# A hybrid encoder's first stage: the sample's projection taken on x * w, with rstd at the readout

## The chip, the cores and the metric

The kernel runs on one core of a Trainium2 chip. The metric is device time in microseconds (us) of the whole kernel. Five engines work from queues of their own, each in program order: TensorE (PE, matrix products), VectorE (DVE), ScalarE (ACT), GpSimd (POOL) and SyncE (SP), which issues most DMAs. They wait for each other by semaphores. TensorE writes its sums into PSUM banks; all other tiles lie in SBUF, "on chip" below.

## The reference

Two requests share one set of weights: a prompt of 1024 tokens and a sample of 256 tokens, each of width 1024. One layer follows: a token-mixing block, cross-attention into 256 memory tokens, and a feed-forward part. Only the start of the first block matters here:

```
h = rmsnorm(x, norm_mix_w)            # x * rsqrt(mean(x*x) + eps) * w
proj = h @ w_in                       # split into qkv, ab, dn_gate, sg_u, sg_v, gate_a, gate_b
u = gelu(sg_u); v = layernorm(gelu(sg_v))
y_b = (u * (w_s @ v + b_s)) @ w_up_b  # w_s mixes the tokens of a chunk of 128
```

`rsqrt(mean(x*x) + eps)` is one number per token, called rstd here. It can be applied to `x` before the product or to the product's rows after it.

## The kernel before

Tokens form three blocks: 0 and 1 are the two halves of the prompt (512 tokens each), 2 is the sample (256 tokens). A chunk is 128 tokens. Activations lie with features on the partitions: a tile `x[:, k, :]` is 128 features by the block's tokens, `k` from 0 to 7 (`KT` = 8).

Every product is made of three: both operands are split into a rounded high part and the remainder (`hi`, `lo`), and `hi*hi`, `lo*hi` and `hi*lo` are summed in one bank. `split` (L124) makes the high part on ACT (L125) and the remainder on DVE or POOL (L126). For weights the two parts are `svh`/`svl` (the `w_sv` halves) and `whi`/`wlo` (all the others); `raw` is a weight tile as loaded.

The stage around the change runs in this order on TensorE:

- `sgv(2)`, the sample's columns `sg_v` and `ab`: two halves of the weight (264 columns each), two chunks, 24 products of 264 columns for each pair: 96 in all.
- `bias()`, one product that needs the small tile `sw`.
- `sgu(0, 2)` and `sgu(1, 2)`, the sample's first two groups of `sg_u`: 24 products of 256 columns each.
- `sgv(0)`: the same as `sgv(2)` for the four chunks of block 0, 192 products; then `sgu(0, 0)` and `sgu(1, 0)`, 24 products of 512 columns each; then `sgv(1)`, and so on.

The norms run beside it. A norm squares `x` on ACT (L240, L243), adds the squares on DVE (L244, the tile `nacc`), sums over the partitions with products of one column (`bank<-cst,nacc`), takes rsqrt on DVE in three rounds of three small instructions (L226 to L228, the tile `nst`), spreads the result over the partitions with products of 128 columns (`bank<-cst,nst`), and then for each `k` multiplies on DVE (L276, the tile `nt`) and splits into `hi` and `lo` (L287: odd `k` have their remainder on DVE, even `k` on POOL). `nt` and the squares share three rooms. After each readout of a bank, `gelu2` (L400) runs ACT, DVE, ACT, DVE in turn.

The order on TensorE is written out by hand, with generators: the main one emits products, and side ones (the norms, the layer norm `ln`, the mixing products) are resumed when a planned clock, advanced by each product's planned time, reaches a due time. `LAG0` is such a time: how far behind the start of block 0's norm its column sums are placed. The other engines get their order from a scheduler within the same program. `x` of block 1 is loaded into the room of block 0's `x`, so its load waits for the last `nt` of block 0.

Of the kernel before, what the change touches and what calls it, by code (L numbers as in the profile page):

```python
# [54 lines left out]
class Trunk:  # L55
# [68 lines left out]
    def split(self, hi, lo, src, eng=None):  # L124
        self.nc.scalar.activation(hi, src, AF.Copy)  # L125
        (eng or self.nc.vector).tensor_tensor(out=lo, in0=src, in1=f32(hi), op=ALU.subtract)  # L126
# [37 lines left out]
def trunk_kernel(ctx: ExitStack, tc: tile.TileContext, a):  # L164
# [122 lines left out]
    def to_h(h, b):  # L287
        return lambda k, t: split(h[b][0][:, k, :], h[b][1][:, k, :], t, V if k % 2 else G)

    def act_tiles(p=None):  # L290

        p = p or hp
        return [
            (
                p.tile([P, KT, n], F32R, tag=f"hi{b}", name=f"hi{b}"),
                p.tile([P, KT, n], F32R, tag=f"lo{b}", name=f"lo{b}"),
            )
            for b, (_, n) in enumerate(BLOCKS)
        ]
# [29 lines left out]
            SY.dma_start(x[:, k : k + 2, :], src[:, k : k + 2, t0 : t0 + n])  # L329
        return x  # L330

    def sv_raw(half):
        raws = [K.raw() for _ in range(2)]
        for i, raw in enumerate(raws):
            SY.dma_start(raw, a["w_sv"][half][:, i * 1056 : (i + 1) * 1056])
        return raws

    def sv_split(half, raws):
        lo = svp.tile([P, 8 * 264], F32R, tag="lo", name="svl")
        hi = svp.tile([P, 8 * 264], F32R, tag="hi", name="svh")  # L340
        for i, raw in enumerate(raws):
            sl = slice(i * 1056, (i + 1) * 1056)
            split(hi[:, sl], lo[:, sl], raw, V if i else G)
        sv.append((hi, lo))


    xs = hp.tile([P, KT, NS], F32, tag="lo1", name="xs")
    for k in range(0, KT, 2):
        SY.dma_start(xs[:, k : k + 2, :], a["xT"][:, k : k + 2, NP:])
    SY.dma_start(sm, a["small"])  # L350
    SY.dma_start(cst[:, C_BD:], a["const"][:, C_BD:])
    sv_raw0 = sv_raw(0)
    SY.dma_start(cst[:, :C_BD], a["const"][:, :C_BD])
    x_h = act_tiles()

    def first_norm():

        nm = Norm(xp, 512)
        for k in range(0, KT, 2):
            nm.add(xs[:, k : k + 2, :].rearrange("p k t -> p (k t)"))  # L360
        nm.n = NS
        yield from nm.rest(lambda k: xs[:, k, :], S_MIX, to_h(x_h, 2), 0, lag=0, halves=2)

    first = K.side(first_norm())
    sv_split(0, sv_raw0)
    x0 = x_load(a["xT"], 0, 512, "x0")
    sv_split(1, sv_raw(1))
    K.finish(first)

    done = set()  # L370

    def other_norms():
        yield from norm(xp, lambda k: x0[:, k, :], 512, S_MIX, to_h(x_h, 0), 600, 0, LAG0)
        done.add(0)
        x1_ = x_load(a["xT"], 512, 512, "x1")
        yield 3000
# [62 lines left out]
    def decays():  # L439
# [46 lines left out]
            tr(pt[:, d * 40 : (d + 1) * 40], gr[:, d, :], ident[:40, :40])  # L486
        V.tensor_copy(gcol.rearrange("p d r -> p (d r)"), pt[:, :80])

    def sgv(b):
        if b < 2:  # L490
            K.until(norms, lambda: b in done)
        for half in (0, 1):
            w = sv[half]
            nv = 264 if half == 0 else 248
            for c in range(4 * b, min(4 * b + 4, NCH)):
                cs = slice((c % 4) * P, (c % 4 + 1) * P)
                hi, lo = x_h[b]
                ps = bank(pm)
                n = 0
                for k in range(KT):  # L500
                    wh, wl = wk(w, k, 264)
                    for l, r in ((hi[:, k, cs], wh), (lo[:, k, cs], wh), (hi[:, k, cs], wl)):
                        mm(ps[:, :264], l, r, n == 0, n == 23)
                        n += 1
                    yield 0
                acc = (s0 if half == 0 else s1)[:, c : c + 1]
                gelu2(sp, ps[:, :nv], vg[:, c, half * 264 : half * 264 + nv], nv, acc)
                if half:
                    V.tensor_copy(ab[:, c, :], ps[:, 248:264])
        lns[b] = K.side(ln(slice(4 * b, min(4 * b + 4, NCH))))  # L510
        K.ahead()

    def bias():
# [23 lines left out]
    def sgu(g, b):  # L537
# [10 lines left out]
        gelu2(sp, ps, ug, n)  # L548
        mixes.append(K.side(mix(g, b, ug)))

    for b in (2, 0, 1):
# [6 lines left out]
        K.main(sgu(1, b))  # L558
    for g in (2, 3):
        for b in (2, 0, 1):  # L560
            K.main(sgu(g, b))
# [1553 lines left out]
```

## Time and profile before

| what | us |
|---|---|
| median of 3 runs | 2263.11 |
| lowest and highest run | 2262.23, 2266.95 |
| the profiled execution | 2267.29 |
| its span in the trace | 2265.1 |
| TensorE busy in the span | 2204.3 |
| start of the first product with `w_sv` | 15.04 |
| block 0's rstd spread over the partitions (`bank<-cst,nst`) | 37.31 |
| block 1's column sums (`bank<-cst,nacc`) | 64.53 |
| start of `sgv(1)` | 87.04 |

Times in the trace are counted from the span's start. A row of the timeline gives start, duration, engine, line, operation, out<-in with partitions and elements, and the count of merged instructions; in brackets stands how long the engine was idle before it, and who ended that.

### The profile page before, as it was taken

The numbers are of one execution on the slowest core, as the hardware profiler recorded it, in microseconds if no ns is written. First come the engines' busy times: TensorE is split into PE (matmuls) and PEld (weight loads), VectorE is DVE, ScalarE is ACT, GpSimd is POOL, SyncE is SP. The second block draws the span as 40 slices with busy tenths as digits, with TensorE's granted clock in tenths as the row PEclk, the third lists the DMA queues.
The fourth block names the chain that finished last, engine by engine and source line by source line (L and its number), as shares of the span: only waits on it lengthen the run. The fifth ranks groups of instructions, "written<-read, shape, count | busy, mean of one in ns | idle before, by whom it ended". The sixth has DMA issues, their size and how long they took to land.

```text
span 2265.1 us, 32398 instructions
## 1 busy us (share of the span) xinstructions
PE 2204.3 (97%) x12464; PEld 1923.5 (85%) x12464; DVE 1396.8 (62%) x2774; ACT 815.7 (36%) x1480; POOL 527.5 (23%) x352
## 2 busy tenths in 40 slices
PE   6999999999999999999999999899999999999998
PEld 6988888888888898888888888788888888878888
DVE  7868778897985964664534547543344334468575
ACT  5433243333424433232344423323233222343453
POOL 3010000000000000013221331566666666100031
PEclk9999999999999999999999999899999999999999
DMA  5221322223234555962231431223222222593531
GB/s 186 83 82 62 105 66 85 78 65 98 73 110 125 158 140 166 308 227 94 91 101 47 163 131 59 72 82 114 78 79 89 75 82 75 167 346 110 198 110 56
DMA packets 191301, 262.47 MB, mean 116 GB/s; under 512 B 72410, under 2 KB 102698, under 8 KB 191146
## 3 DMA queue, kind: packets, MB, share of 16 engines
q1 hardware_dynamic: 171306, 231.30, 31.6%
q10 hardware_dynamic: 19840, 29.11, 3.5%
q8 instruction: 97, 1.59, 0.3%
q14 instruction: 58, 0.48, 0.1%
HBM read 182.19 MB, written 78.16 MB: 115 GB/s over the span
## 4 chain that ended last, share of the span: by engine, by line
PE 79%; DVE 9%; DMA 4%; issue 4%; ACT 2%; POOL 1%; SPq 0%; ACTq 0%; POOLq 0%; DVEq 0%
PE bank L108 78%; DMA tbd<-stage 1%; PE bank L121 1%; DVE acc L591 1%; DVE wlo L126 1%; DVE W L737 1%; DMA braw<-gq 1%; DVE nt L276 0%; DVE sw L895 0%; DVE W L740 0%; DMA gb<-grd 0%; DVE U L837 0%; DMA t<-sgd 0%; DVE lo L126 0%; DMA stage<-gtd 0%
## 5 line engine op out<-in xcount | busy, mean ns | idle before, releaser
L108 PE MATMUL bank<-hi,whi 128*128 128x512 f32 (+1 forms) x2144 | 765.3, 357 | 2.7 <-ACT whi L125 1.6
L108 PE MATMUL bank<-lo,whi 128*128 128x512 f32 (+1 forms) x2144 | 750.5, 350 | 1.1 <-POOL lo L126 1.1
L108 PE MATMUL bank<-hi,wlo 128*128 128x512 f32 (+1 forms) x2144 | 750.2, 350 | 0.9 <-DVE wlo L126 0.9
L108 PEld LDWEIGHTS bank<-hi,wlo 128*128 128x128 f32 x2144 | 407.3, 190 | 55.3 <-DVE wlo L126 1.4
L108 PEld LDWEIGHTS bank<-hi,whi 128*128 128x128 f32 x2144 | 408.1, 190 | 52.8 <-ACT whi L125 2.1
L108 PEld LDWEIGHTS bank<-lo,whi 128*128 128x128 f32 x2144 | 408.2, 190 | 50.1 <-POOL lo L126 1.4
L126 POOL TENSOR_TENSOR wlo<-raw,whi 128x1024 fp32r<-128x1024 f32 x70 | 178.6, 2555 | 377.9 <-ACT whi L125 221.1
L125 ACT ACTIVATE whi<-raw 128x1024 fp32r<-128x1024 f32 (+1 forms) x135 | 140.8, 1043 | 176.4 <-PE bank L108 129.8
L108 PE MATMUL bank<-bhl,whi 128*128 128x512 f32 x456 | 140.6, 389 | 0.0
L126 POOL TENSOR_TENSOR wlo<-room,whi 128x1024 fp32r<-128x1024 f32 x42 | 100.6, 2396 | 116.1 <-ACT whi L125 114.2
L108 PEld LDWEIGHTS bank<-bhl,whi 128*128 128x128 f32 x456 | 85.5, 188 | 17.8
L1779 DVE TENSOR_TENSOR room<-room,bank 128x512 f32<-128x512 f32 x21 | 14.5, 688 | 131.8 <-ACT room L1559 131.8
L125 ACT ACTIVATE whi<-room 128x1024 fp32r<-128x1024 f32 x42 | 44.6, 1061 | 141.7 <-PE bank L108 138.9
L126 DVE TENSOR_TENSOR wlo<-raw,whi 128x1024 fp32r<-128x1024 f32 (+1 forms) x65 | 77.0, 1185 | 29.6 <-ACT whi L125 27.6
L108 PE MATMUL bank<-bhl,wlo 128*128 128x512 f32 x228 | 88.8, 390 | 1.3 <-DVE wlo L126 1.3
L591 DVE SCALAR_TENSOR_TENSOR acc<-craw,sm,acc 128x510 f32<-128x510 f32 (+1 forms) x96 | 73.6, 767 | 22.3 <-ACT acc L589 20.8
L737 DVE TENSOR_TENSOR W<-W,UT 128x2 f32<-128x2 f32 (+30 forms) x155 | 73.0, 471 | 11.5 <-DMA W<-in_eye 7.2
L243 ACT ACTIVATE nsq<-x 128x512 f32<-128x512 f32 (+1 forms) x70 | 40.2, 584 | 102.4 <-DVE x L1229 91.1
L244 DVE TENSOR_TENSOR nacc<-nacc,nsq 128x512 f32<-128x512 f32 (+1 forms) x73 | 55.3, 758 | 34.0 <-ACT nsq L243 32.8
L954 ACT ACTIVATE gs<-bank 128x512 f32<-128x512 f32 (+1 forms) x60 | 31.2, 520 | 125.3 <-PE bank L108 120.0
L1581 DVE SCALAR_TENSOR_TENSOR t<-bank,t 128x512 f32<-128x512 f32 (+1 forms) x44 | 24.5, 558 | 81.9 <-PE bank L108 81.9
L857 POOL COPY UT<-U 64x512 f32<-64x512 f32 x20 | 13.8, 697 | 246.7 <-PE bank L108 245.1
(342 smaller groups left out, 4266.7 us busy)
## 6 DMA issues: line engine op xcount, KB each, us to landing
raw<-in_w_gu SPq DMA_DIRECT2D x44, 512.0 KB, 3.8
braw<-gq SPq DMA_DIRECT2D x14, 1024.0 KB, 6.4
raw<-in_w_g SPq DMA_DIRECT2D x20, 512.0 KB, 3.3
gq<-t SPq DMA_DIRECT2D x33, 256.0 KB, 2.0
gtd<-gs ACTq DMA_DIRECT2D x32, 256.0 KB, 2.0
w<-in_w_dn SPq DMA_DIRECT2D x8, 1024.0 KB, 9.1
raw<-in_w_qkv SPq DMA_DIRECT2D x12, 512.0 KB, 3.6
gq<-r SPq DMA_DIRECT2D x22, 256.0 KB, 4.5
```

The lines of the kernel that those rows point to most:

```text
L108: self.nc.tensor.matmul(out, l, r, start=start, stop=stop, skip_group_check=more)
L121: self.nc.tensor.transpose(out, x, ident)
L125: self.nc.scalar.activation(hi, src, AF.Copy)
L126: (eng or self.nc.vector).tensor_tensor(out=lo, in0=src, in1=f32(hi), op=ALU.subtract)
L243: S.activation(sq, x, AF.Square)
L244: (eng or V).tensor_tensor(out=self.acc, in0=self.acc, in1=sq, op=ALU.add)
L591: V.scalar_tensor_tensor(out=dst, in0=src, scalar=wj, in1=dst, op0=ALU.mult, op1=ALU.add)
L737: V.tensor_tensor(out=t3, in0=u3[:, i:, c:].rearrange("p j c -> p c j"), in1=XL[:, 32 * i + i : 32 * i + 32].unsqueeze(1).to_broadcast([P, ...
L857: G.tensor_copy(Um[q, hs, :], U[d][q, hs, :])
L954: S.activation(t, ps, AF.Tanh, scale=0.5)
L1581: V.scalar_tensor_tensor(out=out, in0=u, scalar=sign, in1=t, op0=ALU.mult, op1=ALU.mult)
L1779: V.tensor_tensor(out=c22, in0=c22, in1=pe, op=ALU.add)
```

## The change

What it does, in the order of the program:

- **Loads.** `sm`, the column of ones and the identity are loaded from ACT's queue. On SP the sample's `x` comes in four pieces with the first half of `w_sv` in two pieces between and behind them; then the second half of `w_sv`, which now has a room of its own (`svraw`, in the later room of `hi0`) instead of waiting for the first half's; then the first tile of `w_u`, block 0's `x`, and the second tile of `w_u`, both in rooms that lie in the later `lo1` (the tile `xs` in the listings).
- **x * w first.** For the sample the first projection takes `xw`, that is `x * w` split into `hi` (ACT, with a scale) and `lo` (DVE, one instruction with `xs` and `hi` as its inputs). The 96 products of `sgv(2)` use it, in a new order: per half of the weight and per half of the `k`, all products with `svh`, then all with `svl`.
- **Squares.** The sample's squares aren't added on DVE: each pair of `k` goes to TensorE as 4 products of one column, 16 in all, accumulated in two banks.
- **rstd at the readout.** `y0` holds the sample's rstd. `sgv_out` multiplies each bank in place by it on ACT (L531) ahead of the gelu.
- **The sample's normalised x** is still needed from `sgu` on. It is made by `first_norm`, which now spreads `y0` in the middle of `sgv(2)`.
- **Groups of three.** `sgv(0)` takes chunks 0, 1 and 2 of the first half of the weight together, `k` by `k`; the rest chunk by chunk as before.
- **Places.** `bias()` comes after `sgu(1, 2)`; `LAG0` goes from 7500 to 13000.

```diff
+    S.dma_start(sm, a["small"])
+    S.dma_start(cst[:, C_BD:], a["const"][:, C_BD:])
+    S.dma_start(ident, a["const"][:, C_ID : C_ID + P])
+    for half in range(2):
+        xs_load(4 * half)
+        xs_load(4 * half + 2)
+        sv_load(0, half)
+    for i in range(2):
+        sv_load(1, i)
+    SY.dma_start(raw_u[0], a["w_u"][0])
+    x0 = x_load(a["xT"], 0, 512, "x0")
+    SY.dma_start(raw_u[1], a["w_u"][1])
...
     for k in range(0, KT, 2):
...
+        sq = xp.tile([P, 512], F32, tag="nsq", name="nsq", bufs=3)
+        S.activation(sq, xs[:, k : k + 2, :].rearrange("p k t -> p (k t)"), AF.Square)
+        for i in range(2):
+            hi, lo = (xw[:, x, k + i, :] for x in range(2))
+            S.activation(hi, xs[:, k + i, :], AF.Copy, scale=sm[:, S_MIX + k + i : S_MIX + k + i + 1])
+            V.scalar_tensor_tensor(out=lo, in0=xs[:, k + i, :], scalar=sm[:, S_MIX + k + i : S_MIX + k + i + 1], in1=f32(hi), op0=ALU.mult, op1=ALU.subtract)
+        for c in range(2):
+            for i in range(2):
+                mm(pcs[c][:, :1], sq[:, i * NS + c * P : i * NS + (c + 1) * P], one, k + i == 0, k + i == KT - 1)
+        if k % 4 == 2:
+            sv_split(0, k // 4, sv_raws[0][k // 4])
...
+    rsqrt(y0, ms, sc)
+    sv_tiles()
+    for i in range(2):
+        sv_split(1, i, sv_raws[1][i])
...
     def first_norm():
...
+        yield FIRST_N
+        pb = bank()
+        for c in range(2):
+            mm(pb[:, c * P : (c + 1) * P], y0[:, c : c + 1].to_broadcast([P, P]), ident)
+        for k in range(KT):
+            t = xp.tile([P, 512], F32, tag="nsq", name="nt", bufs=3)[:, :NS]
+            V.scalar_tensor_tensor(out=t, in0=xs[:, k, :], scalar=sm[:, S_MIX + k : S_MIX + k + 1], in1=pb[:, :NS], op0=ALU.mult, op1=ALU.mult)
+            to_h(x_h, 2)(k, t)
...
+    def sgv_out(half, c, ps):
+        nv = 264 if half == 0 else 248
+        if c >= 8:
+            S.activation(ps[:, :264], ps[:, :264], AF.Copy, scale=y0[:, c - 8 : c - 7])
+        acc = (s0 if half == 0 else s1)[:, c : c + 1]
+        gelu2(sp, ps[:, :nv], vg[:, c, half * 264 : half * 264 + nv], nv, acc)
...
+        for half, cs in ((0, (0, 1, 2)), (0, (3,)), (1, (0,)), (1, (1,)), (1, (2,)), (1, (3,))) if b == 0 else [(half, (c,)) for half in (0, 1) for c in range(4)]:
...
     for b in (2, 0, 1):
         K.main(sgv(b))
         if b == 2:
-            bias()
+            K.finish(first)
         elif b == 1:
             K.side(decays())
         K.main(sgu(0, b))
         K.main(sgu(1, b))
+        if b == 2:
+            bias()
...
-LAG0, LAGF, LAGF2, PACEF = 7500, (8000, 6000, 1500), (9000, 9000, 2800), 1000
+FIRST_N, LAG0, LAGF, LAGF2, PACEF = 2900, 13000, (8000, 6000, 1500), (9000, 9000, 2800), 1000
```

What stands on the engines shows more than the diff. On DVE, the sample's rsqrt before: the three rounds run in one piece, and only then one `w_sv` remainder follows.

```order
L258 TENSOR_SCALAR bank<-bank 128x2
L224 TENSOR_SCALAR nst<-bank 128x2
L226 SCALAR_TENSOR_TENSOR bank<-nst,bank 128x2
L227 TENSOR_TENSOR bank<-bank,nst 128x2
L228 SCALAR_TENSOR_TENSOR nst<-bank,nst 128x2
...
L228 SCALAR_TENSOR_TENSOR nst<-bank,nst 128x2
L126 TENSOR_TENSOR svl<-raw,svh 128x1056
```

The same place on DVE in the changed kernel (`y_111` is `y0`, L379 the remainder of `x * w`):

```order
L387 TENSOR_SCALAR bank<-bank 128x1 x2
L379 SCALAR_TENSOR_TENSOR xw<-xs,sm,xw 128x256
L224 TENSOR_SCALAR y_111<-bank 128x2
L379 SCALAR_TENSOR_TENSOR xw<-xs,sm,xw 128x256
...
L228 SCALAR_TENSOR_TENSOR y_111<-bank,y_111 128x2
L126 TENSOR_TENSOR svl<-raw,svh 128x1056
...
L228 SCALAR_TENSOR_TENSOR y_111<-bank,y_111 128x2
L126 TENSOR_TENSOR svl<-svraw,svh 128x1056
...
L228 SCALAR_TENSOR_TENSOR y_111<-bank,y_111 128x2
L244 TENSOR_TENSOR nacc<-nacc,nsq 128x512 x5
```

Two remainders of `x * w` and two of `w_sv` have moved in between the rounds. On POOL before, the sample's four remainders (`lo_102`) come between the two of `w_sv`:

```order
L126 TENSOR_TENSOR svl<-raw,svh 128x1056
L126 TENSOR_TENSOR lo_102<-nt,hi_101 128x256 x4
L126 TENSOR_TENSOR svl<-raw,svh 128x1056
L126 TENSOR_TENSOR wlo<-raw,whi 128x1024 x2
L126 TENSOR_TENSOR lo_98<-nt,hi_97 128x512 x4
```

On POOL in the changed kernel:

```order
L126 TENSOR_TENSOR svl<-raw,svh 128x1056
L126 TENSOR_TENSOR svl<-svraw,svh 128x1056
L126 TENSOR_TENSOR wlo<-xs,whi 128x1024 x2
L126 TENSOR_TENSOR lo_177<-nt,hi_176 128x256 x4
L126 TENSOR_TENSOR lo_179<-nt,hi_178 128x512 x4
```

The sample's four (`lo_177`) now stand behind both remainders of `w_u`. On TensorE before, `sgu(0, 2)` has had three products when block 0's rstd is spread (`bank<-cst,nst`, four products), and the other 45 of the two groups follow:

```order
L108 MATMUL bank<-sw,cst 128x512
L108 MATMUL bank<-hi_101,whi 128x256
L108 MATMUL bank<-lo_102,whi 128x256
L108 MATMUL bank<-hi_101,wlo 128x256
L108 MATMUL bank<-cst,nst 128x128 x4
L108 MATMUL bank<-hi_101,whi 128x256
L108 MATMUL bank<-lo_102,whi 128x256
```

On TensorE in the changed kernel first the start, up to the spreading of `y0` (row 5), and then the end of `sgu(1, 2)`:

```order
L108 MATMUL bank<-cst,nsq 128x1 x16
L108 MATMUL bank<-svh,xw 128x264 x16
L108 MATMUL bank<-svl,xw 128x264 x8
L108 MATMUL bank<-svh,xw 128x264 x4
L108 MATMUL bank<-cst,y_111 128x128 x2
...
L108 MATMUL bank<-hi_176,wlo 128x256
L108 MATMUL bank<-cst,nst 128x128 x4
L108 MATMUL bank<-sw,cst 128x512
L108 MATMUL bank<-sw,vg 128x128 x2
L108 MATMUL bank<-svh,hi_178 128x264
```

The spreading of block 0's rstd has moved behind all 48 products of `sgu(0, 2)` and `sgu(1, 2)`, right ahead of `bias()` and `sgv(0)`.

More of the change, by code (lines that the diff above doesn't have):

```diff
@@ L330, in x_load @@
         return x
[L332 to L344, printed above, removed]
@@ L347, in trunk_kernel, with sv_tiles @@
-    xs = hp.tile([P, KT, NS], F32, tag="lo1", name="xs")
-    for k in range(0, KT, 2):
[L349 to L354, printed above, removed]
-    def first_norm():
[L358 to L362, printed above, removed]
+    def sv_tiles():
+        sv.append(tuple(svp.tile([P, 8 * 264], F32R, tag=t, name=f"sv{t[0]}") for t in ("hi", "lo")))
@@ new lines, in sv_split @@
+    def sv_split(half, i, raw):
+        sl = slice(i * 1056, (i + 1) * 1056)
+        hi, lo = sv[half]
+        split(hi[:, sl], lo[:, sl], raw, V if i else G)
+    early = hp.tile([P, 4096], F32, tag="lo1", name="xs")
+    xs = early[:, :2048].rearrange("p (k t) -> p k t", t=NS)
+    raw_u = [early[:, 2048 + 1024 * i : 3072 + 1024 * i] for i in range(2)]
+    xw = hp.tile([P, 2, KT, NS], F32R, tag="hi1", name="xw")
+    sv_raw1 = hp.tile([P, 8 * 264], F32, tag="hi0", name="svraw")
+    sv_raws = [[K.raw(), K.raw()], [sv_raw1[:, :1056], sv_raw1[:, 1056:]]]
@@ L487, in decays @@
         V.tensor_copy(gcol.rearrange("p d r -> p (d r)"), pt[:, :80])
-    def sgv(b):
-        if b < 2:
-            K.until(norms, lambda: b in done)
-        for half in (0, 1):
-            w = sv[half]
[L494 to L504, printed above, removed]
-                    yield 0
[L506 to L510, printed above, removed]
+    def sgv_out(half, c, ps):
[4 more added lines that the diff above has]
+        gelu2(sp, ps[:, :nv], vg[:, c, half * 264 : half * 264 + nv], nv, acc)
+        if half:
+            V.tensor_copy(ab[:, c, :], ps[:, 248:264])
```

51 lines of the change are left out of this document (47 added, 4 removed).

## The prediction

> **What bounds the kernel now.** I read the page first (busy shares, chain), then the chain of waits, then tables by stage, then the timelines of the first 90 us.
>
> ```profile
> PE 2204.3 (97%) x12464; PEld 1923.5 (85%) x12464; DVE 1396.8 (62%) x2774; ACT 815.7 (36%) x1480; POOL 527.5 (23%) x352
> ```
>
> TensorE bounds the kernel. In the chain of waits one piece of its first part reads (start, duration, work):
>
> ```profile
> 50.90 51.07 PE bank L108 x362
> ```
>
> These are 51 us of products without a wait. So whatever the change does must be settled by the time TensorE runs freely, and passes to the end unchanged, because all that follows stands in the same order. The table of stages (busy time of PE, PEld, DVE, ACT, POOL, with counts; then granted clock, DMA share, GB/s) shows what can be won:
>
> ```profile
> 15.04:35.11 20.07, 17.31 (x104) 16.19 (x105) 16.55 (x37) 12.98 (x26) 7.75 (x6) 0.91 0.43 151
> 35.11:43.67 8.56, 7.74 (x61) 7.08 (x59) 7.43 (x20) 4.21 (x9) 5.88 (x4) 1.00 0.42 123
> 43.67:50.90 7.23, 4.65 (x24) 3.21 (x23) 7.17 (x18) 4.28 (x9) 2.93 (x2) 0.81 0.08 6
> 50.90:64.53 13.63, 13.63 (x97) 13.63 (x98) 10.61 (x31) 7.87 (x16) 0.00 (x0) 0.85 0.47 172
> 64.53:87.04 22.51, 22.51 (x147) 20.64 (x146) 17.34 (x58) 14.83 (x32) 5.53 (x4) 1.00 0.27 94
> ```
>
> The rows are sgv(2); the two sample groups of sgu; the start of sgv(0); sgv(0) up to block 1's column sums at 64.53; and from there to sgv(1). The last is full, so I count to 64.53: whatever block 1's sums are later or earlier by, the kernel is.
>
> Products of 264 columns start 0.22 us apart at the low clock and 0.12 at the full one. Four products of one column take eight records, 1.86 us at the start and 0.94 later; spreading block 0's rstd waited 0.82 us:
>
> ```profile
> 28.17 0.42 PE L108 MATMUL bank<-svh,hi 128*128 128x264 f32 x1
> 28.39 0.42 PE L108 MATMUL bank<-svh,lo 128*128 128x264 f32 x1
> ...
> 61.15 0.28 PE L108 MATMUL bank<-svl,hi 128*128 128x264 f32 x1
> 61.27 0.28 PE L108 MATMUL bank<-svh,hi 128*128 128x264 f32 x1
> ...
> 8.54 1.86 PE L108 MATMUL bank<-cst,nacc 128*128 128x1 f32 x8 [8.54 <-DVE nacc L244]
> 37.31 1.13 PE L108 MATMUL bank<-cst,nst 128*128 128x128 f32 x8 [0.82 <-DVE nst L228]
> 64.53 0.94 PE L108 MATMUL bank<-cst,nacc 128*128 128x1 f32 x8
> ```
>
> **Step 1, the start.** ACT and loads:
>
> ```profile
> 3.57 0.63 ACT L240 ACTIVATE nacc<-xs 128x512 f32<-128x512 f32 x1 [1.56 <-DMA xs<-in_xT]
> 5.93 1.40 ACT L243 ACTIVATE nsq<-xs 128x512 f32<-128x512 f32 x2 [0.99 <-DMA xs<-in_xT]
> 9.46 1.08 ACT L125 ACTIVATE svh<-raw 128x1056 fp32r<-128x1056 f32 x1 [2.13 <-DMA raw<-in_w_sv]
> 15.42 0.71 ACT L125 ACTIVATE hi<-nt 128x256 fp32r<-128x256 f32 x2
> 11.00:12.00 1.00, 0.00 (x0) 0.00 (x0) 0.83 (x6) 0.91 (x1) 1.00 (x1) 1.00 1.03 390
> ```
>
> The last sample piece was there by 6.6; half a MB of weights now comes ahead of it (1.4 us at 390 GB/s) and small loads beside it, so about 9. ACT has more per pair: a square (0.63), two copies (0.71), and after the second pair a weight half (1.08). Its third square starts at 9.0 and the fourth ends near 10.8. The last eight one-column products then end at 13.4 (low clock) or 11.8 (full). I take 13.4, since the trace has no full clock before 20 us. The first product with w_sv gains 1.6 us on 15.04. The three adds that leave DVE shorten nothing by themselves: DVE has room there, and the one-column products that replace them stand on TensorE's own path.
>
> ```profile
> 17.39:20.80 3.41, 3.24 (x13) 2.93 (x14) 3.16 (x7) 2.30 (x6) 1.46 (x2) 1.00 0.76 283
> 20.80:24.21 3.41, 3.41 (x29) 3.41 (x29) 2.99 (x5) 3.41 (x6) 0.20 (x1) 1.00 0.01 5
> ```
>
> Rule and row differ here. In the rows the count per stretch doubles only at 20.8, 5.8 us after the first product with w_sv, although the one-column products had begun at 8.54. The Trainium skill, "TensorE: Matmul & The Clock Gate", Part 1, gives some 3.4 us of sustained matmuls as enough; by it the earlier squares would open the clock, these products end at 11.8, and the sum below be 1.6 us less.
>
> **Step 2, the wait for y0.** TensorE meets the spreading of y0 after 28 products (0.12 to 0.22 each), near 17.
>
> ```profile
> 10.62 2.41 POOL L126 TENSOR_TENSOR svl<-raw,svh 128x1056 fp32r<-128x1056 f32 x1 [10.18 <-ACT svh L125]
> 10.84 0.17 DVE L226 SCALAR_TENSOR_TENSOR bank<-nst,bank 128x2 f32<-128x2 f32 x1
> 11.04 0.17 DVE L227 TENSOR_TENSOR bank<-bank,nst 128x2 f32<-128x2 f32 x1
> 12.52 1.63 DVE L126 TENSOR_TENSOR svl<-raw,svh 128x1056 fp32r<-128x1056 f32 x1
> 27.43 1.25 DVE L126 TENSOR_TENSOR svl<-raw,svh 128x1056 fp32r<-128x1056 f32 x1
> 33.23 4.71 POOL L126 TENSOR_TENSOR wlo<-raw,whi 128x1024 fp32r<-128x1024 f32 x2 [6.27 <-ACT whi L125]
> ```
>
> From the sums at 13.4, DVE has two small ones (0.4), two remainders of x * w (0.4 each), a guess (0.2), three rounds of 0.6 and two w_sv remainders (1.25): 18.9 if nothing interferes. But POOL works at the same time. DVE's remainder, begun at 12.52, took 1.63 and ended 1.12 after POOL's op did (13.03), where it takes 1.25 alone: it stood still until POOL was done. Now POOL runs its second w_sv remainder from about 13.6 to 16.0. DVE's first follows (to 17.3), then a round, while POOL has begun w_u's (2.36, to 19.6); DVE's second ends at 20.8, y0 at 21.4. If a remainder of x * w is caught too, 23.2. I take 22: TensorE idles some 5 us. Between the ends 18.9 and 23.2 the row of 12.52 decides for the upper part.
>
> The row shows this standing still only for L126. The Trainium skill, "SBUF — State Buffer", Who interferes with whom, extends it to any DVE instruction with two SBUF inputs against a GpSimd op that reads SBUF, so to L379; by it y0 would be at 23.2 and the sum 1 us more, by the row alone at 21.4 and 1 us less.
>
> **Step 3, the rest of sgv(2).** The spreading (0.6) and 68 products at 0.12 (8.2) follow, with one stretch at the low clock after such a gap:
>
> ```profile
> 44.69:48.11 3.42, 2.03 (x12) 1.40 (x11) 3.42 (x7) 2.41 (x5) 2.26 (x2) 1.00 0.00 0
> 48.11:51.52 3.41, 2.22 (x8) 1.41 (x7) 3.31 (x11) 0.94 (x2) 0.67 (x1) 0.51 0.27 40
> 51.52:54.93 3.41, 3.41 (x17) 3.41 (x17) 2.72 (x9) 2.29 (x5) 0.00 (x0) 0.50 1.06 403
> ```
>
> With 1.4 us idle in the first stretch the clock was half in the next two. One such stretch costs 1.7 us: sgv(2) ends at 32.5, against 35.11. That counts as won what TensorE lost before by w_sv's second half, which had to wait for the first half's room and now has its own:
>
> ```profile
> 27.02 0.39 PE L108 MATMUL bank<-svl,hi 128*128 128x264 f32 x1 [1.98 <-POOL svl L126]
> ```
>
> The readout's scaling adds four ACT instructions (about 0.39, as other reads of these banks), beside TensorE. The loads that SP now issues ahead of block 0's x (two more w_sv parts and a w_u tile, 1.6 MB, 4 us at 390 GB/s) delay its squares to 16 to 21, where nothing asks for them before step 4; they cost nothing as long as y0 is later than that, and stand first in the way if it isn't.
>
> **Step 4, the sample's norm and sgu.** Rows for the sample's remainders and for a readout of sgu:
>
> ```profile
> 15.07 0.73 POOL L126 TENSOR_TENSOR lo<-nt,hi 128x256 fp32r<-128x256 f32 x1 [2.04 <-ACT hi L125]
> 19.42 1.31 DVE L126 TENSOR_TENSOR lo<-nt,hi 128x256 fp32r<-128x256 f32 x2
> 45.68 0.37 ACT L402 ACTIVATE gt<-bank 128x256 f32<-128x256 f32 x1
> 46.08 0.42 ACT L404 ACTIVATE gt<-gt 128x256 f32<-128x256 f32 x1
> 46.62 0.41 DVE L405 SCALAR_TENSOR_TENSOR ug<-gt,bank 128x256 f32<-128x256 f32 x1
> ```
>
> It used to be done ahead of sgv(2); now the two groups of sgu wait for it, and w_sv's products cover it only if it is early. It isn't. ACT reads out the first bank at about 25.5 (16 products after y0's spreading), between squares of block 0; DVE's first nt stands behind an add and a gelu op of that chain (29 to 30), and POOL's w_u remainder (2.36), whose ACT half stands behind a tanh, comes ahead of the sample's. First lo at 33.5; eight tiles took 5.7 us before (first and second row, 15.07 to 20.7), so 39.2. The products trail them: first group to 41, second 24 * 0.12 = 2.9 plus 1 us of low clock to 45. Before: 43.67. Of the 2.6 us nothing is left, 1.3 are lost.
>
> **Step 5, block 0's rstd.** Before, it was spread at 37.31 with 45 products behind it that covered the first nt. Now it stands behind all 48, and its last DVE steps behind the second group's gelu ops (the last three rows above): ACT 0.37, DVE 0.41, tanh 0.42, DVE 0.41, a step 0.2, so 1.8 us idle, and spread at 47: 9.7 later. That cover's price is this whole step.
>
> **Step 6, block 0's nt and block 1's sums.**
>
> ```profile
> 38.48 2.07 DVE L276 SCALAR_TENSOR_TENSOR nt<-x,sm,bank 128x512 f32<-128x512 f32 x3 [0.39 <-PE bank L108]
> 50.15 0.69 DVE L126 TENSOR_TENSOR lo<-nt,hi 128x512 fp32r<-128x512 f32 x1
> 49.48 1.92 SPq L329 DMA_DIRECT2D x<-in_xT x4
> 62.49 0.69 DVE L244 TENSOR_TENSOR nacc<-nacc,nsq 128x512 f32<-128x512 f32 x1
> ```
>
> From spreading to the last lo took 13.5 us (37.31 to 50.84). With bias and layer-norm ops now inside, I take 14: 61. Groups of three do their work here: the 7.23 us stage, half idle, is covered. But block 1's load starts with the last nt, at 60 instead of 49.48, and only 9 + 24 + 10 products (5.2 us) are left ahead of its column sums. From issue to last add it took 13.7 us (49.48 to 63.18), part of it behind gelu ops; the load alone needs 7.2 (2.1 MB at 403 GB/s, and 2 us ahead of the first bytes, by the stretches above), with two squares (0.63) and an add 9.2. I take 12, so 72 for the last add and 72.3 for the sums; TensorE gets there at 66 and idles 6 us.
>
> **The sum.** 72.3 - 64.5 = 8 us later, rounded: +9.7 to the spreading of block 0's rstd (steps 1 to 5), +0.8 from there to block 1's load (13 for 12.2), -2.7 from the load to the sums (12.3 for 15.05). The profiled execution (2267.29) lies 4.2 above the median, so I add 8 to the median: 2271.1. Its own range goes from y0 at 18.9 with a kinder ACT order, +5, to every end unfavourable with two more low-clock stretches, +13: 2268 to 2276.
>
> **The rivals.**
> - A draw. DVE does not stand still for POOL, or loads land a microsecond or two earlier: y0 at 17 to 19, sgu's end at 38 to 41, block 0's rstd at 40 to 42.5, block 1's sums at 64 to 67.5: 0 to +3 us, 2263 to 2266. For it: starts of POOL and DVE may miss each other. Against: POOL has four remainders of 2.4 us almost in a row.
> - Faster. TensorE spent 35.9 us from 15.04 to 50.90 on about 170 products, worth some 22 at the full clock; the change can win that slack if the sample's norm is ready when sgv(2) ends. It decides if block 0's rstd is spread before 35: then sums at 60, -4.5 to -8, about 2257. For it: the earlier start. Against: steps 2 and 4, each of which uses up more than the 1.6 us of step 1.
> - The change doesn't do what it says: the projection should no longer wait for rstd, but y0's spreading sits 28 products into it. That is in the forecast; were y0 free, step 2 gives 5 us back and the draw results.
>
> **How the numbers follow.** 0.2% is 4.5 us, about what a measurement can tell from no change: 2258.6 to 2267.6. Chances: the forecast with its own range 0.57, worse than it 0.06, the draw 0.20, faster 0.17. So slower 0.63, same 0.20, faster 0.17. The range takes in the draw and its edges, 2259 to 2277.
>
> **What would show it.** In the changed kernel's timeline: a TensorE wait for y0 of some 5 us near 17; DVE's two w_sv remainders longer than 1.25 or late behind POOL's; TensorE waiting for lo in sgu(0, 2); block 0's spreading near 47; a wait for nacc of 4 to 6 us in sgv(0); sgv(1) starting near 95 instead of 87.04. It is wrong if y0 comes before 18, or if block 0's spreading stands below 40.

## The result, and where the time went

The changed kernel takes 2274.14 us (2274.06 to 2274.89), the kernel before 2262.67 beside it: 1.0051 times as long, with a 95% interval from 1.0038 to 1.0063. That is 11.5 us slower; 2271.1 was forecast. Run a second time, beside the last experiments, it gave 2276.26 against 2263.75, a ratio of 1.0052 (1.0038 to 1.0066).

The first line of the page of the changed kernel hardly differs, since the loss is small against the whole:

```profile
PE 2210.2 (97%) x12488; PEld 1930.9 (85%) x12488; DVE 1401.7 (62%) x2780; ACT 818.8 (36%) x1492; POOL 525.9 (23%) x352
```

The loss lies between the first product with `w_sv` and `sgv(1)`. One row of the table of stages for that stretch, of the kernel before and then of the changed one (its length, busy time of PE, PEld, DVE, ACT, POOL with counts, granted clock, DMA share, GB/s):

```profile
15.04:87.04 72.00, 65.84 (x426) 60.74 (x427) 59.10 (x159) 44.17 (x92) 22.09 (x15) 0.93 0.35 119
```

```profile
13.44:97.34 83.90, 70.57 (x432) 66.39 (x431) 65.03 (x176) 44.38 (x97) 21.13 (x15) 0.88 0.30 107
```

The work is nearly the same (432 records of products for 426), and the changed kernel starts it 1.6 us sooner. It takes 11.9 us more: TensorE is idle for 13.3 us instead of 6.2, and busy 4.7 us longer at a lower clock (0.88 for 0.93). The clock is recorded from 20.88 on in the kernel before and from 18.80 on in the changed one; ahead of that its column reads 1.00 in all the tables, though products of 264 columns start some 0.22 us apart there, the pace of the low clock. TensorE's idle time by what ended it, the five largest rows from the table of waits for the same stretch of the changed kernel (us in total, times, longest):

```profile
PE bank L108 <- DVE nacc L244: 3.6, 1, 3.6
PE bank L108 <- DVE vg L473: 3.2, 1, 3.2
PE bank L108 <- DVE y L228: 2.8, 1, 2.8
PE bank L108 <- POOL lo L126: 1.9, 2, 1.7
PE bank L108 <- DVE nst L228: 1.5, 1, 1.5
```

And the places in its timeline, in order:

```profile
9.87 3.57 PE L108 MATMUL bank<-cst,nsq 128*128 128x1 f32 x16 [1.68 <-ACT nsq L375]
...
22.24 1.22 PE L108 MATMUL bank<-cst,y 128*128 128x128 f32 x4 [2.82 <-DVE y L228]
...
34.59 0.39 PE L108 MATMUL bank<-lo,whi 128*128 128x256 f32 x1 [1.72 <-POOL lo L126]
...
48.25 1.16 PE L108 MATMUL bank<-cst,nst 128*128 128x128 f32 x8 [1.46 <-DVE nst L228]
...
53.47 1.20 PE L108 MATMUL bank<-sw,vg 128*128 128x128 f32 x4 [3.20 <-DVE vg L473]
...
61.18 1.92 SPq L329 DMA_DIRECT2D x<-in_xT  x4
...
72.85 1.32 PE L108 MATMUL bank<-cst,nacc 128*128 128x1 f32 x8 [3.62 <-DVE nacc L244]
...
78.65 1.05 PE L108 MATMUL bank<-cst,nst 128*128 128x128 f32 x8
...
140.61 1.59 PE L108 MATMUL bank<-sw,vg 128*128 128x128 f32 x6 [1.32 <-DVE vg L473]
148.26 1.05 PE L108 MATMUL bank<-sw,vg 128*128 128x128 f32 x8
```

| event | before | after | later by |
|---|---|---|---|
| first product with `w_sv` (after: end of the squares) | 15.04 | 13.44 | -1.6 |
| block 0's rstd spread | 37.31 | 48.25 | 10.9 |
| block 1's load | 49.48 | 61.18 | 11.7 |
| block 1's column sums | 64.53 | 72.85 | 8.3 |
| block 1's rstd spread | 68.69 | 78.65 | 10.0 |
| `sgv(1)` | 87.04 | 97.34 | 10.3 |
| eight mixing products of block 1 | 136.41 | 148.26 | 11.85 |

The medians, 11.5 us apart, show nothing more lost behind the last row. That the two spans (2265.1 and 2272.3) differ by only 7.2 us comes from the profiled execution of the kernel before, which lies 4.6 us above its median: a loaded tile came later there, and TensorE then waited 1.78 us and had half the clock from 283.70 to 290.53.

```profile
248.89 0.16 DVE L737 TENSOR_TENSOR W<-W,UT 128x2 f32<-128x2 f32 x1 [4.90 <-DMA W<-in_eye]
...
281.41 1.02 PE L108 MATMUL bank<-cst,gs 128*128 128x1 f32 x8 [1.78 <-DVE vw L763]
```

In the changed kernel the same wait for `W` was 2.77 us and TensorE did not wait. I therefore compare traces up to the eight mixing products, and whole times by their medians.

### The profile page after: what moved, and what is told of

It reads as the page before. It is cut to its first block, busy times and chain, and to the rows that moved or that the text cites. A ratio compares the mean times of both kernels' runs of the same rounds, so it can differ in the third digit from the quotient of the medians.

```text
span 2272.3 us, 32464 instructions
## 1 busy us (share of the span) xinstructions
PE 2210.2 (97%) x12488; PEld 1930.9 (85%) x12488; DVE 1401.7 (62%) x2780; ACT 818.8 (36%) x1492; POOL 525.9 (23%) x352
## 4 chain that ended last, share of the span: by engine, by line
PE 81%; DVE 8%; DMA 4%; issue 4%; ACT 2%; POOL 1%; SPq 0%; ACTq 0%; POOLq 0%; DVEq 0%
PE bank L108 80%; DMA tbd<-stage 1%; PE bank L121 1%; DVE wlo L126 1%; DMA braw<-gq 1%; DVE acc L655 1%; DVE sw L959 0%; DMA gb<-grd 0%; DMA stage<-gtd 0%; DVE U L901 0%; ACT whi L125 0%; ACT nsq L243 0%; DVE nacc L244 0%; DVE nt L276 0%; DMA raw<-in_w_sv 0%
## 5 line engine op out<-in xcount | busy, mean ns | idle before, releaser
L126 POOL TENSOR_TENSOR wlo<-raw,whi 128x1024 fp32r<-128x1024 f32 x68 | 173.7, 2557 | 371.4 <-ACT whi L125 371.4
L1293 DVE SCALAR_TENSOR_TENSOR x<-bank,x 128x512 f32<-128x512 f32 (+1 forms) x48 | 28.6, 599 | 71.2 <-PE bank L108 67.7
```

The source lines that it names most:

```text
L1293: V.scalar_tensor_tensor(out=x[b][:, m, :], in0=ps, scalar=scale, in1=x[b][:, m, :], op0=ALU.mult, op1=ALU.add)
```

## The experiments

Ratios are to the kernel before, run on the same chip. The changed kernel stands at 1.0051 and 1.0052 there, and 0.0010 is 2.3 us. The intervals reach 2 to 3.3 us to either side, so smaller differences are read from the traces.

### y0: is TensorE's wait the loss, and why is y0 late?

```diff
-            mm(pb[...], y0[:, c : c + 1].to_broadcast([P, P]), ident)
+            mm(pb[...], one.to_broadcast([P, P]), ident)
```

> The spreading on TensorE, 28 products into the sample's first projection, takes a column of ones in place of y0; so rstd is left out of the sample's gated rows (not of the projection's readout), and TensorE has nothing to wait for there. Theory (a chain: the readout of the first bank, the sample's nt and lo, sgu's two groups and block 0's last rsqrt steps all follow one another): the wait of 2.82 us at 19.4 is gone and all that follows comes about 2.8 us earlier: block 0's spreading at 45.5 instead of 48.25, block 1's sums at 70 instead of 72.85, 2271.3 us, give or take 1.7 for a stretch at the low clock. Rival (the draw of the prediction: with y0 free 5 us come back): 2269 or less. Second rival (later waits take it up, since block 0's squares or POOL's w_u remainder hold the sample's lo where it is): within 1 us of 2274.

Measured: 2272.97 us, ratio 1.0039 (1.0024 to 1.0054). From its timeline:

```profile
44.82 1.16 PE L108 MATMUL bank<-cst,nst 128*128 128x128 f32 x8 [1.46 <-DVE nst L228]
...
69.58 1.83 PE L108 MATMUL bank<-cst,nacc 128*128 128x1 f32 x8 [3.81 <-DVE nacc L244]
76.73 1.05 PE L108 MATMUL bank<-cst,nst 128*128 128x128 f32 x8
```

The chain is as the theory has it: the spreading comes 3.4 us earlier and block 1's sums 3.3. But the wait at those sums stays, and the stretch at the low clock behind it is longer (7.15 us from sums to spreading instead of 5.80), so 1.9 us are left at block 1's spreading. The rival of 5 us fell; of the second rival, later waits, a part is true.

The second run leaves `y0` in and takes away what POOL reads while DVE works on it.

```diff
+        if half and not i:
+            S.activation(hi[:, sl], raw, AF.Copy)
+            G.memset(f32(lo[:, sl]), 0.0)
+            return
         split(hi[:, sl], lo[:, sl], raw, V if i else G)
```

and the same for the first tile of `w_u`.

> GpSimd's remainder of the first part of w_sv's second half and that of the first w_u tile are replaced by filling those tiles with zeros (they are left out of the computation), so that POOL reads nothing from SBUF between 12 and 30; the order on TensorE, VectorE and ScalarE stays. Theory (VectorE's two-input ops stand still while POOL reads): the last remainder of x * w takes 0.5 us instead of 2.67, VectorE's first w_sv remainder 1.25 instead of 2.97, y0 is ready at 18.2 to 19 instead of 22.18 and TensorE doesn't wait for it; then all as with y0 free: block 0's spreading about 3 us earlier, 2271 to 2273 in the end. Rival (VectorE was late for another reason, loads or ScalarE): both ops stay above 2 us and y0 stays at 21 to 22.

Measured: 2269.35 us, ratio 1.0019 (1.0008 to 1.0031). By the ratios this is 7.2 us back, more than the theory gave it; in the trace the eight mixing products come 3.7 us sooner (144.58). DVE and POOL in the changed kernel:

```profile
13.96 2.46 POOL L126 TENSOR_TENSOR svl<-svraw,svh 128x1056 fp32r<-128x1056 f32 x1 [2.17 <-ACT svh L125]
14.03 2.67 DVE L379 SCALAR_TENSOR_TENSOR xw<-xs,sm,xw 128x256 fp32r<-128x256 f32 x1
16.36 2.59 POOL L126 TENSOR_TENSOR wlo<-xs,whi 128x1024 fp32r<-128x1024 f32 x1
17.09 2.97 DVE L126 TENSOR_TENSOR svl<-raw,svh 128x1056 fp32r<-128x1056 f32 x1
20.45 1.26 DVE L126 TENSOR_TENSOR svl<-svraw,svh 128x1056 fp32r<-128x1056 f32 x1
22.02 0.16 DVE L228 SCALAR_TENSOR_TENSOR y<-bank,y 128x2 f32<-128x2 f32 x1
```

and with POOL quiet (the same instructions, a few lines further down in the code):

```profile
13.83 0.48 DVE L387 SCALAR_TENSOR_TENSOR xw<-xs,sm,xw 128x256 fp32r<-128x256 f32 x1
14.69 1.26 DVE L126 TENSOR_TENSOR svl<-raw,svh 128x1056 fp32r<-128x1056 f32 x1
17.91 0.16 DVE L232 SCALAR_TENSOR_TENSOR y<-bank,y 128x2 f32<-128x2 f32 x1
```

Two DVE instructions that overlap POOL's take 2.67 and 2.97 us, and 0.48 and 1.26 without it. Each ends some 0.3 to 1.1 us after POOL's op, so DVE stood still. `y0` is there 4.1 us sooner, and TensorE's spreading at 19.31 waits for nothing. This is the cause of step 2, and it applies to L379 too, as the Trainium skill, "SBUF — State Buffer", Who interferes with whom, has it for two SBUF inputs against a GpSimd op that reads.

### Is the lost cover behind block 0's spreading the price?

```diff
-FIRST_N, LAG0, LAGF, LAGF2, PACEF = 2900, 13000, ...
+FIRST_N, LAG0, LAGF, LAGF2, PACEF = 2900, 10000, ...
```

> Block 0's column sums and the spreading of its rstd are put ahead of sgu's two sample groups (LAG0 10000 in place of 13000), so that the groups' 48 products stand behind the spreading again, as 45 of them did before the change. Theory (the price is that lost cover): block 0's sums are met as soon as its last add is done (31), its rsqrt steps no longer stand behind the second group's gelu, the spreading comes at 36 to 38 instead of 48.25, block 1's load at 49 to 51 instead of 61.18, its sums at 62 to 65 instead of 72.85: 8 to 11 us back, 2263 to 2266. Rival (VectorE is the bound between 28 and 40, and block 0's steps only push the sample's nt and lo out by as much): 3 us or less back, 2271 to 2275.

Measured: 2269.95 us, ratio 1.0029 (1.0017 to 1.0040): 5 us back, between the theory and the rival, with the spreading at 42.79 and block 1's load at 58.26. The text on record is wrong about the edit: only the sums stood ahead of `sgu`'s groups, the spreading between them. So a second run put it ahead of both:

```diff
-FIRST_N, LAG0, LAGF, LAGF2, PACEF = 2900, 13000, ...
+FIRST_N, LAG0, LAGF, LAGF2, PACEF = 2900, 7500, ...
```

> LAG0 7500: block 0's sums stand 31 products ahead of the end of the sample's projections, the spreading of its rstd right ahead of sgu's 48 sample products. (With 10000 only the sums were ahead of them, the spreading stood between the two groups.) Theory A (the lost cover is the price): spreading at 38 to 39, block 1's load at 51 to 52, its sums at 64 to 66: 7 to 9 us back, 2265 to 2267. Theory B (since the spreading at 42.79 with 10000 brought the load only to 58.26: VectorE's work between 28 and 60 is the bound, and its order only shifts who is late): load at 56 or later, 4 us back or less, 2270 or more.

Measured: 2271.69 us, ratio 1.0038 (1.0025 to 1.0050). Its timeline:

```profile
30.63 1.05 PE L108 MATMUL bank<-cst,nacc 128*128 128x1 f32 x8 [1.73 <-DVE nacc L244]
40.75 2.08 PE L108 MATMUL bank<-cst,nst 128*128 128x128 f32 x8 [5.81 <-DVE nst L228]
54.79 0.59 PE L108 MATMUL bank<-svh,hi 128*128 128x264 f32 x1 [3.60 <-DVE ug L444]
69.35 0.95 PE L108 MATMUL bank<-cst,nacc 128*128 128x1 f32 x8
```

The spreading comes 7.5 us sooner, and block 1's load too (52.36 for 61.18, as theory A has it). Still only some 3 us come back by the ratios (0.0013, within what the intervals leave open), the size of theory B, and 3.1 us in the trace (eight mixing products at 145.14). TensorE now waits 1.73 us for block 0's sums, 5.81 for its rstd, whose rsqrt steps share DVE with the sample's `nt` and `lo`, and 3.60 for a bank, and reaches block 1's sums 3.5 us sooner instead of 7 to 9. The idle time has moved, not gone. That the cover's price is the whole of the 9.7 us, as step 5 puts it, has fallen: the cover alone doesn't bring them back.

### Block 1's sums

```diff
-        yield 3000
+        yield 7000
         yield from norm(xp, lambda k: x1_[:, k, :], 512, S_MIX, to_h(x_h, 1), 900)
```

> Block 1's column sums stand 36 products later in sgv(0) (the pause ahead of its norm 7000 in place of 3000), with nothing else moved ahead of them; the sums of the third norm move along. Theory: TensorE doesn't wait at 69.2 (3.62 us) and has no stretch at the low clock behind it (1.66 us); the spreading of block 1's rstd comes at 77.8 where it was 78.65, so sgv(1) doesn't wait either: 5 us back, 2269. Rival (block 1's lo are then late for sgv(1), and the wait only moves): 0 to 1 us, 2273 to 2274.

Measured: 2269.33 us, ratio 1.0033 (1.0019 to 1.0047). No wait at the sums, and no low clock behind them:

```profile
73.15 1.02 PE L108 MATMUL bank<-cst,nacc 128*128 128x1 f32 x8
77.39 1.05 PE L108 MATMUL bank<-cst,nst 128*128 128x128 f32 x8
```

From sums to spreading 4.24 us instead of 5.80, and 36 more products are done by then. The eight mixing products come at 143.65, 4.6 us sooner than in the changed kernel, and the ratios give 4.1 us back, near the 5 of the theory. The profiled execution itself took 2276.20 us, the slowest of five, so its trace is used only up to those products.

```diff
-FIRST_N, LAG0, ... = 2900, 13000, ...
+FIRST_N, LAG0, ... = 5000, 13000, ...
-        yield 3000
+        yield 7000
```

> Two moves on TensorE alone: the spreading of y0 stands 18 products later (FIRST_N 5000), so that it finds y0 ready, and block 1's sums stand later as in the run with 7000. Theory (the 2.8 us for y0 pass through once nothing waits at block 1's sums): no wait for y0, none at block 1's sums, sgv(1) 2.8 to 3.4 us earlier than with the sums moved alone: 2266 to 2266.5. Rival (as with y0 free alone, half of it is lost again behind): 2268 to 2269.

Measured: 2268.56 us, ratio 1.0018 (1.0003 to 1.0032), with runs from 2263.9 to 2276.2. The wait for `y0` shrinks to 1.08 us, but the next grows:

```profile
22.01 0.71 PE L108 MATMUL bank<-cst,y 128*128 128x128 f32 x4 [1.08 <-DVE y L228]
...
32.30 0.58 PE L108 MATMUL bank<-lo,whi 128*128 128x256 f32 x1 [2.66 <-POOL lo L126]
...
46.76 1.16 PE L108 MATMUL bank<-cst,nst 128*128 128x128 f32 x8 [1.46 <-DVE nst L228]
```

The spreading is only 1 us sooner than with the sums moved alone (47.73). Meeting `y0` later helps little while `y0` itself is late. The runs scatter too much to say by the times whether 0.8 us (medians) or 3.4 (ratios) were won. The trace speaks for the rival: the eight mixing products come at 145.37, later than with the sums moved alone (143.65), since three stretches at the low clock lie ahead of them behind block 1's rstd, where the other trace has one.

### The groups of three

First alone, in the kernel before:

```diff
+        for half, cs in ((0, (0, 1, 2)), (0, (3,)), (1, (0,)), (1, (1,)), (1, (2,)), (1, (3,))) if b == 0 else ...
...
+            for k in range(KT):
...
+                for c, p in zip(cs, ps):
```

> The kernel before with one part of the change alone: the first three token groups of sgv(0) share each piece of w_sv and run through the pieces together. Theory (block 1's load sets the time): the half idle stage from 43.67 to 50.90 fills up and TensorE reaches block 1's sums 3 to 4 us sooner, but the last add of its squares is done at 63.18 as before, so it waits there: 0 to 1.3 us won, 2261.4 to 2262.7. Rival (the groups by themselves win the idle time of that stage): 4 us or more, 2258.5 or less.

Measured: 2265.00 us, ratio 1.0005 (0.9996 to 1.0015).

```profile
47.10 0.39 PE L108 MATMUL bank<-svh,hi 128*128 128x264 f32 x1 [2.53 <-DVE ug L405]
...
63.66 1.02 PE L108 MATMUL bank<-cst,nacc 128*128 128x1 f32 x8 [0.27 <-DVE nacc L244]
```

Three banks at once have to wait for a readout (2.53 us), and block 1's sums move by 0.9 us, after a wait for the last add. Nothing is won that a measurement can tell.

Then the changed kernel without them:

```diff
-        for half, cs in ((0, (0, 1, 2)), (0, (3,)), ...) if b == 0 else [...]:
+        for half, cs in [(half, (c,)) for half in (0, 1) for c in range(4)]:
```

> The changed kernel without the groups of three: sgv(0) takes one token group at a time, as before. Theory (block 1's load sets the end of this part, as with the groups alone in the kernel before): block 1's load and the last add of its squares stay, TensorE idles between 54 and 62 instead of at 69, and its sums stay at 72 to 73: within 1.5 us of 2274. Rival (the groups do their work, as step 6 has it): 3 us or more slower, 2277 and up.

Measured: 2272.51 us, ratio 1.0035 (1.0023 to 1.0046).

```profile
43.43 1.16 PE L108 MATMUL bank<-cst,nst 128*128 128x128 f32 x8 [1.46 <-DVE nst L228]
...
69.82 0.95 PE L108 MATMUL bank<-cst,nacc 128*128 128x1 f32 x8
73.97 1.05 PE L108 MATMUL bank<-cst,nst 128*128 128x128 f32 x8
```

From block 0's spreading to block 1's it took 30.54 us, in the changed kernel 30.40: the groups neither win nor lose. The rival (3 us slower) fell, and the sums stood 3 us earlier than the theory had them. That comes from ahead of `sgv(0)`, where the two kernels have the same instructions in the same order. From block 0's sums to its spreading, first in the changed kernel, then in this one:

```profile
39.57:48.25 8.68, 7.22 (x36) 7.02 (x35) 4.27 (x28) 3.29 (x9) 0.00 (x0) 0.62 0.00 1
```

```profile
37.69:43.43 5.74, 4.28 (x37) 4.08 (x35) 4.49 (x29) 3.30 (x9) 0.00 (x0) 1.00 0.00 1
```

The same products took 2.9 us more at a granted clock of 0.62 than at 1.00. The wait for the sample's first `lo` ahead of them was shorter here as well (1.10 us for 1.72), so these rows don't say whether its length or where it fell decided the clock.

### The causes together

The changed kernel itself, beside the next three:

> The changed kernel as it is, beside the three that follow, since its runs and those of the other experiments were on chips whose runs scatter differently. Theory: 11.5 us over the kernel before, as first measured, 2274 to 2276 where before has 2263 to 2265. If the low clock in sgu's second group is chance in the phase of the clock's windows (the kernel without groups of three had block 0's spreading at 43.43 after the same instructions in the same order): runs down to some 4 us below that.

Measured: 2276.26 us (2273.16 to 2277.63), ratio 1.0052 (1.0038 to 1.0066). None of its runs came down by 4 us, and its profiled execution again had the low clock in `sgu`'s second group (spreading at 47.80). The half clock began there at 35.72, in the first profile at 35.87, at nearly the same place of the program; what another place would give isn't shown by these two.

Next a version that leaves nothing out:

```diff
+        if half and not i:
+            G.tensor_copy(lo[:, :2], y0)
         split(hi[:, sl], lo[:, sl], raw, V if i else G)
...
+            if j == 0:
+                self.nc.gpsimd.tensor_copy(lo[:, :2], self.hold)
             self.split(hi, lo, self.raws.pop(j), ...)
...
-        yield 3000
+        yield 7000
```

> Nothing is left out: POOL starts its remainder of w_sv's second half and that of the first w_u tile only when y0 is there (a copy of two columns from y0 into each tile ahead of it), and block 1's sums stand 36 products later, as in the earlier run. Theory (the two causes add up: the standing still of VectorE costs 4 to 5 us, the wait at block 1's sums with its low clock 5): y0 at 18, no wait for it, none at block 1's sums, 2264 to 2265.5 where the changed kernel has 2274. Rival (they are one loss, counted twice, since each only moves idle time that TensorE spends elsewhere): 2268 or more.

Measured: 2267.21 us, ratio 1.0011 (1.0002 to 1.0020): 9.0 us less than the changed kernel beside it. That is the 8.5 to 10 of the theory; its absolute times were too low, since the changed kernel itself ran 2 us higher here. By the medians the rival, which allowed 6 us, fell. That the two add up in full is not shown: the ratio with POOL quiet alone (1.0019) lies within the interval, and in the trace the eight mixing products come at 143.04, 5.2 us sooner than in the changed kernel, where the runs alone have 3.7 and 4.6. This profiled execution, at 2270.46 us, lies 3.3 above its median. Its spreading of `y0` at 19.06 and block 1's sums at 71.30 wait for nothing.

Then the same with `bias()` in its old place:

```diff
             K.finish(first)
+            bias()
...
-        if b == 2:
-            bias()
```

> As the run before it, with the bias back ahead of sgu, where it stood before the change. Theory: VectorE's four bias ops and the layer norm no longer share the time behind the spreading, block 0's last rsqrt steps no longer stand behind the second group's gelu, and TensorE's wait of 3.2 us for the mixing product goes: 1 to 3 us less than without it, 2262 to 2264, level with the kernel before. Rival (VectorE has the same work either way, the wait moves into sgv(0)): within 1 us of the run without it.

Measured: 2263.56 us, ratio 0.9998 (0.9990 to 1.0007): 3.6 us less again, and level with the kernel before. The eight mixing products come at 136.97, in the kernel before at 136.41.

```profile
41.35 1.05 PE L108 MATMUL bank<-cst,nst 128*128 128x128 f32 x8
...
48.54 0.85 PE L108 MATMUL bank<-sw,vg 128*128 128x128 f32 x4 [0.35 <-DVE vg L478]
```

```profile
13.30:85.46 72.16, 66.29 (x431) 61.74 (x431) 62.38 (x164) 40.83 (x90) 22.58 (x17) 0.93 0.28 99
```

Block 0's spreading finds its rstd ready, the wait for the mixing product is 0.35 us instead of 3.20, and the stage has about the idle time (5.9 us for 6.2) and the clock (0.93) of the kernel before. The rival fell. But the edit moves more than `bias()`, since the side generators follow the planned clock: block 0's sums now stand behind 12 of `sgu`'s 48 products and its spreading behind 39, where it was 21 and 48, and the mixing product behind the last nine and the first of `sgv(0)`. Whether VectorE's bias ops or these places won the 3.6 us was not separated.

Last, `bias()` as changed and `LAG0` 10000 on top of the version with POOL late:

> As the run with POOL late and block 1's sums later, with LAG0 10000: block 0's sums ahead of sgu's two sample groups, the spreading between them. Theory (block 0's nt come earlier, and nothing behind takes it back): 1 to 3 us less than with 13000, 2262 to 2264. Rival (VectorE is the bound there, as the run with LAG0 10000 alone showed): within 1 us of it.

Measured: 2265.03 us, ratio 1.0006 (0.9997 to 1.0015), 2.2 us less than without it. The size is the theory's, but the intervals of the two overlap: that block 0's sums, put earlier, help once `y0` is early is likely, not shown. No version beat the kernel before by an amount that can be told from none.

## Why the prediction was right, and where its sum was short

- **What bounds the kernel.** It was settled ahead of `sgv(1)` and passed on to the end: 10.3 us there, 11.5 by the medians.
- **Step 1** held: the squares ended at 13.44, at the low clock.
- **Step 2** held in cause: `y0` at 22.18, forecast 22. Two DVE instructions stood still, but not the pair of the forecast: an `x * w` remainder and the first `w_sv` remainder did, and the last `w_sv` remainder ran alone (1.26). The forecast had two `w_sv` remainders (21.4) or all three (23.2) and took a value between, so that it came this close is in part luck. Its terms without standing still add up to 19.1, not 18.9. The wait was 2.8 us, not 5: step 2 put TensorE's arrival near 17, the full clock's pace, but the 28 products ahead took 0.22 us each, up to 19.4.
- **Steps 3 and 4** held: `sgv(2)` ended at 32.8 (32.5), DVE's first `nt` came at 29.86, the first group ended at 42.1 (41), with block 0's sums among its last products. The second group ended late, at 46.8 instead of 45: nearly all of it ran at the low clock.
- **Step 5** had the place right, 48.25 for 47, and the mechanism: the last rsqrt steps stood behind a gelu op that waited for TensorE's second group (row below). But its sentence "That cover's price is this whole step" failed: putting the cover back won 3 to 5 us by the ratios, since DVE could not finish block 0's rstd in time for the earlier place. What helped were other changes: with POOL late it was spread at 44.83, still after a wait of 1.46 us, and with `bias()` in its old place besides at 41.35, without a wait. How much of the second is `bias()` itself stays open, since block 0's sums moved with it.

```profile
47.30 0.42 DVE L442 SCALAR_TENSOR_TENSOR gt<-gt,bank 128x256 f32<-128x256 f32 x1 [3.28 <-ACT gt L441]
47.64 0.16 DVE L227 TENSOR_TENSOR bank<-bank,nst 128x4 f32<-128x4 f32 x1
```

- **Step 6** held: load at 61.18 (60), 12.9 us after the spreading (13); sums at 72.85 (72.3), after a wait of 3.6 us (6). A wait of 3.2 us for the mixing product, which it had not named, held TensorE back on the way. Its sentence "Groups of three do their work here" failed: without them the same stretch took as long, for TensorE idled at one end of it or the other until block 1's load was done. (The stage of 7.23 us that they were to cover was idle for 2.6 us, not half of it.)
- **The sum.** Up to block 1's sums it was +8 and measured 8.3. The step that failed is "whatever block 1's sums are later or earlier by, the kernel is": the wait itself closed the clock behind it. From sums to spreading took 5.80 us instead of 4.16 (1.6 more). Another 0.6 us went by 138.24 (127.71 before), most of it in a wait for the third norm's rstd of 0.80 us instead of 0.35. The last 1.3 us went behind a wait of 1.32 us (140.61) that the kernel before has as well: only the changed kernel then had the half clock, from 141.68 to 145.09. This makes the 3.5 us between 8.3 and 11.85. With the sums moved, the wait and the 1.6 us went together, which supports that they are one.
- **The rivals.** The draw's condition, `y0` at 17 to 19, was made true by quieting POOL and gave 2269.35, above its 2263 to 2266, since the wait at block 1's sums stayed (3.56 us). By the ratio it is 4.3 us over the kernel before (1.8 to 7.0), where the draw had 0 to 3, and by the trace 8.2 at the eight mixing products. Of the 5 us promised for `y0`, the trace with the column of ones has 1.7 (146.61 for 148.26) and that with POOL quiet 3.7. The faster rival needed block 0's rstd before 35, and no run had that.

What stays open: which of the new order of loads and the squares on TensorE costs or wins anything by itself was not tried; the start won 1.6 us with both. Nor was the share of `bias()` apart from the places that move with it.

## What to carry to other kernels

Taking a scale factor out of the first product frees that product, but not the work that still needs the factor: look for who meets it next, and what the engine that computes it shares with its neighbours in that moment. When a forecast ends in a wait of some microseconds on TensorE, add what the low clock behind it costs, here 1.6 us on a wait of 3.6. An event that is late shows where idle time surfaces; only moving it on the chip tells whether it is the cause.

## What the runs showed of the hardware

The granted clock is recorded in stretches of 3.41 us. In the changed kernel the one from 32.45 holds a single wait of 1.72 us up to 34.59, and the next three, up to 46.11, ran at half clock; the one from 46.11 holds a wait of 1.46 us, and the next ran at the full clock:

```profile
32.45:35.87 3.42, 1.70 (x13) 1.36 (x11) 2.80 (x5) 1.47 (x5) 2.79 (x3) 1.00 0.00 0
35.87:39.28 3.41, 2.90 (x11) 2.44 (x11) 3.40 (x10) 2.41 (x7) 1.46 (x2) 0.50 0.00 0
...
46.11:49.53 3.42, 1.96 (x15) 1.67 (x14) 1.96 (x11) 1.10 (x3) 0.00 (x0) 1.00 0.00 0
```

No fixed amount of idle time follows from this: in the kernel before, the stretch from 44.77 was busy for 2.02 us, more than the last of these, and half clock followed. The Trainium skill, "TensorE: Matmul & The Clock Gate", Part 1, says that the window runs freely, so that the moment at which the clock opens depends on the phase; the traces agree in so far as the first full stretch begins at 18.80 in the changed kernel and at 15.87 in the one without groups of three, which has the same instructions up to there. It names an idle window of some 3.4 us as what closes the clock; here a stretch that was busy for 1.70 us did. The one-column products did not open it: without the groups of three they fill the stretch from 9.04 to 12.46 (counted back from the record) without a gap, and the clock opened only at 15.87, after a stretch of 264-column products. This is the row's side of the question that step 1 left open.

DVE's standing still works both ways. In the version with POOL late, POOL's remainders began at 18.81, after `y0`, and met DVE's adds of block 0's squares:

```profile
18.81 2.99 POOL L126 TENSOR_TENSOR svl<-svraw,svh 128x1056 fp32r<-128x1056 f32 x1
...
18.00 4.35 DVE L246 TENSOR_TENSOR nacc<-nacc,nsq 128x512 f32<-128x512 f32 x3
```

Three adds took 4.35 us, which took 2.28 in the changed kernel, and POOL's op 2.99 for 2.46. TensorE didn't wait for either there. The changed kernel has one more such place, which no version took away: the sample's first remainder on DVE took 1.98 us (0.42 for the next, at 35.76), beside POOL's second remainder of `w_u`, and POOL's first `lo` of the sample, for which TensorE waits those 1.72 us, comes behind that.

```profile
31.30 2.38 POOL L126 TENSOR_TENSOR wlo<-xs,whi 128x1024 fp32r<-128x1024 f32 x1 [12.35 <-ACT whi L125]
31.98 1.98 DVE L126 TENSOR_TENSOR lo<-nt,hi 128x256 fp32r<-128x256 f32 x1
```
